# A bidirectional state scan whose matrix products go to TensorE in uncut groups on 64-row tiles, with the second direction's heads swapped

## The chip, the cores and the metric

The kernel runs on one core of a Trainium2 chip. The metric is the device time of one execution in microseconds. A core has a matrix engine (TensorE, "PE" in the profile, its weight loads "PEld"), a vector engine (DVE), a scalar engine (ACT), GpSimd (POOL), a queue engine that starts most transfers (SP), DMA engines, on-chip memory SBUF and the accumulators of TensorE, PSUM, which the program takes in banks of 512 float32 per partition.

## The reference

Two layers over 256 context and 512 latent tokens of width 1024. Layer 0 runs global attention and, beside it, bidirectional RWKV-7 time mixing on 8 heads of width 64; layer 1 runs windowed attention and a Mamba-2 scan; each layer ends with an MLP. Only layer 0's mixing stage matters here. Per head (64 wide) the time mixing runs this step over the tokens:

```
def step(S, inp):
    r_t, w_t, k_t, v_t, kk_t, a_t = inp
    sa = jnp.einsum('bhvk,bhk->bhv', S, kk_t)
    S = (S * w_t[:, :, None, :] - sa[..., None] * (kk_t * a_t)[:, :, None, :]
         + v_t[..., None] * k_t[:, :, None, :])
    return S, jnp.einsum('bhvk,bhk->bhv', S, r_t)
```

once forward and once backward (the context's final state is the latent tokens' first), with weights of its own per direction; the two `y` are added, normalised per head and gated. The attention beside it is the usual one: scores, softmax, the probabilities times the values, all in float32.

## The kernel before, in words

The recurrence is cut into chunks of 32 tokens, two chunks make a block of 64, so there are 12 blocks and 24 steps. Both directions (d = 0 forward, d = 1 backward) run through the same step, and the 8 heads lie as four pairs: pair index a = 0..3, and in a pair head h = 0 on partitions 0–63 and h = 1 on 64–127.

`prepare(b)` loads a block's operands by DMA (SP's queue: `arD` to `ari`, L958; `kbD` to `kbd`, L961; `vD` to `vm`, L965). In its `run()`, called piece by piece, each of four half-blocks (d, m) makes `z`: four matmuls of 128 rows by 128 columns (L985), one for each of two pairs and two chunks. The weights `kbd` are block-diagonal: each of the two heads' 64x64 blocks stands on its own 64 rows and 64 columns, the rest is zeros that were written once (L908/L910). DVE masks `z` twice (L991: `zk`, used for `xv`, and the first half of `z`, used for `y`), ACT copies the other half (L994). Then come two products `xv` (L1002) per block, from `zk` and `vm`, and POOL makes `ard` from `ari` by a decay factor, once per head (L976).

`step` is the recurrence: `x` = `ard` times `state` (L1026), `xs` = `x` + `xv` on DVE (L1029), `u` = the chunk's 32x32 triangular inverses `tt` times `xs` (L1036), `vu` = masked `u` + `vm`, twice on DVE (L1041), `s` = `z` times `vu` (L1051), new `state` = `s` + decayed old state on DVE (L1059). `outputs` makes `y` from `ard` times `state` (L1070) and `z` times `vu` (L1072), and adds it to `yacc`. `ard` and `zk` carry zeros or masks for the head that does not take part, so `x`, `xv` and `y` use all 128 rows and 64 columns: direction 0 on columns 0–63, direction 1 on 64–127.

Every matmul names the part of TensorE's array that it uses by rows, columns and a position: 128x128 (`z`, the scores `sc`, the transposes `pt`), 128x64 at two column positions (`xv`, `x`, `y`, `po`), 64x64 at two positions (`s`) and 32x32 at four (`u`). In float32 the trace shows two records for each such matmul and one for a transpose.

The attention of layer 0 is the other work of the stage. `attend` (L1127 on) loads `qr`, splits it into `qs` (L1136 ACT, L1137 DVE), makes scores (L1147) and probabilities (ACT L1154, L1156). `weighted` (L323, also used by layer 1's attention) transposes the probabilities four heads at a time into a bank (`pt`, L332), copies them to SBUF (`pts`, alternately DVE L335 and ACT L337) and multiplies with the values (`po`, L341).

`state_mixing` drives it: step and outputs of the recurrence, and between them pieces of `prepare` for the next block and of the attention. The order on each engine is then set by a scheduler that takes ready instructions by priority; the recurrence and the first block's preparation are issued under `tc.high_priority()`. So matmuls of one product need not stand together on TensorE: another product's can come between them.

The stage has eight PSUM banks: two for `z`, `xv` and `y` together (tag `zy`), one for `x`, `u`, `s` (`ch`), one `po`, two `pt`, two for one `sc` tile. The heaviest code ahead of the stage is the layer's input projection; behind it comes the layer's MLP. The order of these is not touched.

Of the kernel before, what the change touches and what calls it, by code (L numbers as in the profile page):

```python
# [18 lines left out]
P = 128  # L19
# [19 lines left out]
HALVES = (slice(0, 64), slice(64, 128))  # L39

# [36 lines left out]
def constants():  # L77
# [21 lines left out]
    head, slot = p // 64, (p // 32) % 2  # L99
    own = (head[:, None] == np.arange(2)[None, :])[:, :, None]  # L100
    for dr in (0, 1):
        isk = slot == dr
        sgn = np.where(isk, 1.0, -1.0).astype(f)
        if dr == 0:
            inc, exc = t[None, :] >= s[:, None], t[None, :] > s[:, None]
        else:
            inc, exc = t[None, :] <= s[:, None], t[None, :] < s[:, None]
        c.add(f"rmask{dr}", (own * inc[:, None, :] * sgn[:, None, None]).astype(f))
        c.add(f"kmask{dr}", (own * (exc & isk[:, None])[:, None, :]).astype(f))
        c.add(f"sgn{dr}", sgn)  # L110
        c.add(f"umask{dr}", (~isk).astype(f)[:, None])
# [113 lines left out]
def tile_trunk(ctx: ExitStack, tc: tile.TileContext, t: dict, out, cc: Cols, pc: Cols):  # L225
# [96 lines left out]

    def weighted(prob, vt, g, kts, o, pool):  # L323
# [5 lines left out]
        for m, kt in enumerate(kts):  # L329
            pt = psum("pt", "pt")  # L330
            for j in range(4):
                T.transpose(pt[:, P * j:P * j + P], prob[j][:, P * m:P * m + P], ident)  # L332
# [6 lines left out]
            if len(pair) == 2 or m == n - 1:  # L339
                for i, (m_, k_, w_) in enumerate(pair):  # L340
                    T.matmul(po[HALVES[i], :], lhsT=vt[:, k_, r], rhs=w_, start=m_ < 2, stop=m_ + 2 >= n, tile_position=(0, 64 * i))  # L341
# [544 lines left out]
    with ExitStack() as sb:  # L886
        psum_pool(sb, zy=(2, 1), ch=(1, 1), po=(1, 1), pt=(2, 1), sc=(1, 2))
# [25 lines left out]
        kbd = [bq.tile([P, 4, 2, P], F32, name=f"kbd{n}") for n in range(3)]  # L913
        ari = [bq.tile([P, 4, 2, P], F32, name=f"ari{n}") for n in range(3)]

# [4 lines left out]
        ard = [br.tile([P, 4, 2, 2, 64], F32, name=f"ard{n}") for n in range(5)]  # L920
        zts = [br.tile([P, 4, 2, P], F32, name=f"z{n}") for n in range(4)]
        for n in range(3):
            zero(kbd[n].rearrange("p a c n -> p (a c n)"), n > 1)
# [8 lines left out]
        A.activation(func=AF.Copy, out=dds[:, 0:7, 1, :], in_=DD[1][:, :, 6::-1].rearrange("p a n -> p n a"))  # L932
        A.activation(func=AF.Copy, out=dds[:, 7:23, 1, :], in_=DD[1][:, :, 23:7:-1].rearrange("p a n -> p n a"))
# [13 lines left out]
        def prepare(b):  # L947
# [5 lines left out]
            for d in (0, 1):  # L953
# [3 lines left out]
                kb, ar, bd = kbd[n % 3], ari[n % 3], ard[n % 5]  # L957
                nc.sync.dma_start(ar[:, :, :, 0:64], arD[d][i][:, :, c:c + P].rearrange("q a (c n) -> q a c n", c=2))  # L958
                for h in (0, 1):
                    r = HALVES[h]  # L960
                    nc.sync.dma_start(kb[r, :, :, 64 * h:64 * h + 64], kbD[d][i, r, :, c:c + P].rearrange("q a (c n) -> q a c n", c=2))  # L961
                    v = vD[64 * blk[d]:64 * blk[d] + 64, h].rearrange("(j q) a e -> q j (a e)", j=2)
                    for j in (0, 1):
                        s = 32 * (2 * h + d)
                        nc.sync.dma_start(vm[d][s:s + 32, j].rearrange("q a e -> q (a e)"), v[:, 1 - j if d else j, :])  # L965
                ld.append((kb, ar))
# [3 lines left out]
            def run():  # L970
                zks = {}
                for d in (0, 1):
                    kb, ar = ld[d]
                    for h in (0, 1):
                        r = HALVES[h]
                        G.tensor_tensor(out=ars[d][r, :, :, :, 32 * h:32 * h + 32].rearrange("p a c s t -> p (a c) s t"),  # L976
                                        in0=ar[r, :, :, 0:64].rearrange("p a c (s t) -> p (a c) s t", s=2),
                                        in1=dsel[r, b, d].rearrange("p a c -> p (a c)").unsqueeze(2).unsqueeze(3).to_broadcast([64, 8, 2, 32]),
                                        op=ALU.mult)
                    for m in (0, 1):  # L980

                        ps = psum("zy", "z")
                        for a in (0, 1):
                            for c in (0, 1):
                                T.matmul(ps[:, P * (2 * a + c):P * (2 * a + c) + P], lhsT=kb[:, 2 * m + a, c, :], rhs=ar[:, 2 * m + a, c, :],  # L985
                                         start=True, stop=True)
                        pv = ps.rearrange("p (n x) -> p n x", x=P)
                        z = zs[d][:, 2 * m:2 * m + 2].rearrange("p a c x -> p (a c) x")
                        zk = bq.tile([P, 4, 64], F32, tag="zk", name=u("zk"), bufs=4)
                        for dst, c0, nm in ((zk, 32, "kmask"), (z[:, :, 0:64], 0, "rmask")):  # L990
                            V.tensor_tensor(out=dst.rearrange("p n (h t) -> p n h t", h=2),  # L991
                                            in0=pv[:, :, c0:c0 + 32].unsqueeze(2).to_broadcast([P, 4, 2, 32]),
                                            in1=K(f"{nm}{d}").rearrange("p (h t) -> p h t", h=2).unsqueeze(1).to_broadcast([P, 4, 2, 32]), op=ALU.mult)
                        A.activation(out=z[:, :, 64:128], in_=pv[:, :, 64:128], func=AF.Copy, scale=K(f"sgn{d}"))  # L994
                        zks[d, m] = zk
                        yield
                for j in (0, 1):
                    px = psum("zy", "xv")
                    for a in range(4):
# [804 lines left out]
```

## Time and profile before

| what | value |
|---|---|
| time, three executions | 2007.61, 2008.74, 2009.6 us (median 2008.74) |
| the profiled execution's own time | 2009.51 us |
| its span | 2007.7 us, 34218 instructions |
| TensorE busy in the span | 1896.6 us, 94% |
| DVE, ACT, POOL busy | 61%, 42%, 15% |
| mean granted TensorE clock | 0.975 of full speed |

The profiled execution's 2009.51 us are its span plus 1.8 us around it; it lies 0.77 us above the median. In the window of the trace that matters, from about 350 us (the first `z`) to 625 us (the last `y`), TensorE works on the mixing stage; layer 1's attention, which shares `weighted`, lies at 1450–1610 us. A row of a timeline gives start, duration and a group of equal instructions; a row of the groups gives busy time and the mean nanoseconds of one; because matmuls overlap in the array, the distance from one group's start to the next is the time that a group costs, and not the sum of its durations.

### The profile page before, as it was taken

The numbers are of one execution on the slowest core, as the hardware profiler recorded it, in microseconds if no ns is written. First come the engines' busy times: TensorE is split into PE (matmuls) and PEld (weight loads), VectorE is DVE, ScalarE is ACT, GpSimd is POOL, SyncE is SP. The second block draws the span as 40 slices with busy tenths as digits, with TensorE's granted clock in tenths as the row PEclk, the third lists the DMA queues.
The fourth block names the chain that finished last, engine by engine and source line by source line (L and its number), as shares of the span: only waits on it lengthen the run. The fifth ranks groups of instructions, "written<-read, shape, count | busy, mean of one in ns | idle before, by whom it ended". The sixth has DMA issues, their size and how long they took to land.

```text
span 2007.7 us, 34218 instructions
## 1 busy us (share of the span) xinstructions
PE 1896.6 (94%) x13992; PEld 1545.1 (77%) x13992; DVE 1215.2 (61%) x2150; ACT 840.7 (42%) x1419; POOL 294.2 (15%) x291
## 2 busy tenths in 40 slices
PE   6999988899998999999999999899899789999997
PEld 4776756776765998888888889778578488888886
DVE  5567979775677765654544444865687464444445
ACT  3344442555544552232223224544566454333335
POOL 0000014432321520000000002310153120000001
PEclk9999998899998999999999999999999799999998
DMA  9355575742414733344444422212101133333333
GB/s 336 121 166 171 182 228 148 156 89 56 98 44 132 251 107 99 122 124 136 125 125 121 136 84 80 76 53 74 32 1 53 32 95 105 95 92 97 95 97 113
DMA packets 147884, 228.18 MB, mean 114 GB/s; under 512 B 65024, under 2 KB 102288, under 8 KB 147600
## 3 DMA queue, kind: packets, MB, share of 16 engines
q1 hardware_dynamic: 140912, 213.54, 36.1%
q10 hardware_dynamic: 5456, 7.73, 1.1%
q0 software_dynamic: 1360, 4.73, 0.7%
q8 instruction: 110, 1.80, 0.4%
q14 instruction: 46, 0.38, 0.1%
HBM read 200.00 MB, written 25.96 MB: 113 GB/s over the span
## 4 chain that ended last, share of the span: by engine, by line
PE 77%; DVE 9%; DMA 7%; ACT 3%; issue 3%; POOL 1%; SPq 0%; DVEq 0%; POOLq 0%; ACTq 0%
PE m L367 37%; PE win L367 13%; PE po L341 4%; DMA wmod<-in_wmod_dram 4%; PE pt L332 3%; PE z L985 2%; DVE wlo L280 2%; PE sc L1147 2%; PE wout L1718 1%; PE wout L1302 1%; PE s L1051 1%; PE mod L405 1%; PE lora L653 1%; PE z L1560 1%; DVE junk L1319 1%
## 5 line engine op out<-in xcount | busy, mean ns | idle before, releaser
L279 ACT ACTIVATE whi<-wraw 128x1024 fp32r<-128x1024 f32 x214 | 226.4, 1059 | 678.0 <-PE m L367 561.0
L280 DVE TENSOR_TENSOR wlo<-wraw,whi 128x1024 fp32r<-128x1024 f32 x214 | 264.4, 1236 | 212.2 <-ACT whi L279 209.4
L367 PE MATMUL m<-hh,whi 128*128 128x512 f32 (+1 forms) x816 | 239.3, 344 | 4.9 <-ACT relu L1241 2.4
L367 PE MATMUL m<-hl,whi 128*128 128x512 f32 (+1 forms) x816 | 241.2, 343 | 0.2 <-POOL hl L503 0.2
L367 PE MATMUL m<-hh,wlo 128*128 128x512 f32 (+1 forms) x816 | 241.3, 344 | 0.0
L367 PE MATMUL m<-dl,whi 128*128 128x256 f32 (+1 forms) x832 | 240.7, 341 | 0.0
L367 PE MATMUL m<-dh,whi 128*128 128x256 f32 (+1 forms) x832 | 238.6, 342 | 1.7 <-DVE xl L1223 1.6
L367 PE MATMUL m<-dh,wlo 128*128 128x256 f32 (+1 forms) x832 | 239.8, 341 | 0.1
L367 PEld LDWEIGHTS m<-dh,whi 128*128 128x128 f32 x832 | 153.3, 188 | 23.9 <-DVE xl L1223 4.9
L367 PEld LDWEIGHTS m<-hh,whi 128*128 128x128 f32 x816 | 152.1, 188 | 24.7 <-ACT relu L1241 2.8
L471 POOL TENSOR_TENSOR acc<-acc,nsq 128x256 f32<-128x256 f32 x42 | 42.8, 1027 | 865.8 <-ACT nsq L470 861.0
L367 PEld LDWEIGHTS m<-hl,whi 128*128 128x128 f32 x816 | 153.6, 188 | 19.4 <-POOL hl L503 0.4
L367 PEld LDWEIGHTS m<-dl,whi 128*128 128x128 f32 x832 | 153.8, 188 | 19.0
L367 PEld LDWEIGHTS m<-dh,wlo 128*128 128x128 f32 x832 | 153.7, 188 | 18.9 <-DVE wlo L280 0.3
L367 PEld LDWEIGHTS m<-hh,wlo 128*128 128x128 f32 x816 | 153.4, 188 | 19.0 <-DVE wlo L280 0.3
L367 PE MATMUL win<-hl,whi 128*128 128x512 f32 (+1 forms) x512 | 162.3, 348 | 4.7 <-POOL hl L503 3.5
L367 PE MATMUL win<-hh,whi 128*128 128x512 f32 (+1 forms) x512 | 162.3, 362 | 2.7 <-ACT hh L498 2.7
L367 PE MATMUL win<-hh,wlo 128*128 128x512 f32 (+1 forms) x512 | 160.2, 345 | 0.0
L1319 DVE SCALAR_TENSOR_TENSOR junk<-wmod,crow 128x1024 f32<-128x1024 f32 x64 | 78.5, 1226 | 118.5 <-DMA wmod<-in_wmod_dram 117.9
L1223 DVE SCALAR_TENSOR_TENSOR xl<-m,modT,xl 128x512 f32<-128x512 f32 (+1 forms) x144 | 97.4, 686 | 72.3 <-PE m L367 72.3
L367 PEld LDWEIGHTS win<-hh,whi 128*128 128x128 f32 x512 | 95.4, 194 | 33.6 <-issue 15.7
L367 PEld LDWEIGHTS win<-hl,whi 128*128 128x128 f32 x512 | 98.5, 193 | 22.9 <-issue 5.7
(413 smaller groups left out, 3560.0 us busy)
## 6 DMA issues: line engine op xcount, KB each, us to landing
wraw<-in_w_dram SPq DMA_DIRECT2D x136, 512.0 KB, 3.6
wmod<-in_wmod_dram SPq DMA_DIRECT2D x96, 512.0 KB, 4.2
wraw<-in_wout_dram SPq DMA_DIRECT2D x40, 512.0 KB, 3.7
wraw<-in_win_dram SPq DMA_DIRECT2D x35, 512.0 KB, 4.4
arD<-ar SPq DMA_DIRECT2D x8, 768.0 KB, 4.5
kbD<-kb SPq DMA_DIRECT2D x8, 768.0 KB, 6.5
ari<-arD SPq DMA_DIRECT2D x24, 256.0 KB, 3.9
kbd<-kbD SPq DMA_DIRECT2D x48, 128.0 KB, 3.9
```

The costliest lines, as they stand in the source:

```text
L279: A.activation(out=hi, in_=src, func=AF.Copy)
L280: (lo_eng or V).tensor_tensor(out=lo, in0=src, in1=hi.bitcast(F32), op=ALU.subtract)
L332: T.transpose(pt[:, P * j:P * j + P], prob[j][:, P * m:P * m + P], ident)
L341: T.matmul(po[HALVES[i], :], lhsT=vt[:, k_, r], rhs=w_, start=m_ < 2, stop=m_ + 2 >= n, tile_position=(0, 64 * i))
L367: T.matmul(part(ps, s), lhsT=a[:, c], rhs=row(b, k, s), start=first and j == 0 and q == 0, stop=last and j == n - 1 and q == 2)
L405: T.matmul(ps[r:r + 32, :], lhsT=cs[:, k, :], rhs=wm[:, c], start=k == 0, stop=k == KT - 1, tile_position=(0, r))
L471: (V if k == KT - 1 else eng).tensor_tensor(out=at(acc, s), in0=at(acc, s), in1=at(sq, s), op=ALU.add)
L653: T.matmul(ps[s][d][:, 0:s[1]], lhsT=LORA[wname][r, P * p:P * p + P], rhs=src[r, tokens(s)], start=True, stop=True, tile_position=(64 * d, 0))
L985: T.matmul(ps[:, P * (2 * a + c):P * (2 * a + c) + P], lhsT=kb[:, 2 * m + a, c, :], rhs=ar[:, 2 * m + a, c, :], start=True, stop=True)
L1147: T.matmul(ps[:, cols2(s)], lhsT=qs[:, 2 * j + g, :], rhs=kx[:, g, s[0]:s[0] + s[1]], start=m == 0, stop=m == 1)
L1223: V.scalar_tensor_tensor(out=xs, in0=part(ps, s), scalar=mod(l, which, m, s[2]), in1=xs, op0=ALU.mult, op1=ALU.add)
L1319: V.scalar_tensor_tensor(out=junk, in0=wm, scalar=1.0, in1=crow[:, :, v], op0=ALU.mult, op1=ALU.mult, accum_out=modT[:, l, n, v:v + 1])
```

## The change

A helper `group()` is added. A product's matmuls issued through its `put` stand on TensorE one behind another, uncut: after the first, each is issued at high priority and with an order-only dependency on the one before. It is used for `z`, `xv`, `x`, `u`, `s`, `y`, `sc` and, in `weighted`, for the four transposes of one `pt` and for a pair of `po`. Inside a group the operand that is made last comes first (the fourth head's transpose first, direction 1 first, and so on).

The heads of direction 1 are swapped: the operands of (head h, direction d) lie on rows 64·(h XOR d). With that, each product uses only its own 64 rows:

- `z`: 16 matmuls of 64x64, at the four quadrants of the array, in place of 8 of 128x128 for both directions of a half-block m. The directions write two banks, `pz[0]` and `pz[1]`.
- `xv`, `x`, `y`: 16 matmuls (`y`: 32) of 64 rows by 32 columns, at two row and four column positions, in place of 8 (16) of 128x64.
- `u` and `s`: as many as before and of the same tiles, in another order. `y` now runs all of `z` times `vu` first and `ard` times `state` behind it.
- `zk` is gone, `z` has one mask operation; `kb` and `ard` hold no zeros, and the zeroing of `kbd` and `ard` is gone. `kb` is loaded by one DMA per block and direction in place of two; `ard` is loaded by two further DMAs from `arD` and multiplied in place by one POOL operation in place of two. Two small ACT copies of the decay become four.
- PSUM banks: `z` two of its own, one for `xv`, `y` and `yt`, one `ch`, one `po`, one `pt`, two for `sc`. Eight `prob` buffers in place of five, six `ard` of half the width in place of five.

```diff
+    def group():
+        last = []
+        def put(f, *args, **kw):
+            with tc.high_priority() if last else ExitStack():
+                ins = f(*args, **kw)
+            if last:
+                tc.add_manual_dep(ins.ins, last.pop().ins.name, mybir.DependencyInfo(mybir.DependencyClass.NoSync, mybir.DependencyReason.DATA),
+                                  reason="group")
+            last.append(ins)
+        return put
...
-            for j in range(4):
-                T.transpose(pt[:, P * j:P * j + P], prob[j][:, P * m:P * m + P], ident)
+            put = group()
+            for j in (3, 2, 1, 0):
+                put(T.transpose, pt[:, P * j:P * j + P], prob[j][:, P * m:P * m + P], ident)
...
-        psum_pool(sb, zy=(2, 1), ch=(1, 1), po=(1, 1), pt=(2, 1), sc=(1, 2))
+        psum_pool(sb, z=(2, 1), zy=(1, 1), ch=(1, 1), po=(1, 1), pt=(1, 1), sc=(1, 2))
...
-        for n in range(5):
-            zero(ard[n].rearrange("p a c s n -> p (a c s n)"), n > 1)
...
-                    nc.sync.dma_start(kb[r, :, :, 64 * h:64 * h + 64], kbD[d][i, r, :, c:c + P].rearrange("q a (c n) -> q a c n", c=2))
+                nc.sync.dma_start(kb.rearrange("q a c n -> q a (c n)"), kbD[d][i][:, :, c:c + P])
...
+                for h in (0, 1):
+                    nc.sync.dma_start(bd[HALVES[h ^ d]].rearrange("q a c s t -> q a (c s t)"), arD[d][i, HALVES[h], :, c:c + P])
...
-                        ps = psum("zy", "z")
-                                T.matmul(ps[:, P * (2 * a + c):P * (2 * a + c) + P], lhsT=kb[:, 2 * m + a, c, :], rhs=ar[:, 2 * m + a, c, :],
-                                         start=True, stop=True)
+                    pz = [psum("z", "z") for _ in (0, 1)]
+                    put = group()
+                            for h, d in HD[::-1]:
+                                put(T.matmul, pz[d][HALVES[h ^ d], w:w + P], lhsT=kb[HALVES[h], 2 * m + a, c, :], rhs=ar[HALVES[h], 2 * m + a, c, :],
+                                             start=True, stop=True, tile_position=(64 * h, 64 * (h ^ d)))
...
-                        T.matmul(px[64 * d:64 * d + 64, 64 * a:64 * a + 64], lhsT=ars[d][:, a, cl[d], 1, :], rhs=state[:, d, a, :],
-                                 start=True, stop=True, tile_position=(0, 64 * d))
+                    for h, d in HD:
+                        q = 2 * d + h
+                        put(T.matmul, px[32 * q:32 * q + 32, 64 * a:64 * a + 64], lhsT=ars[d][HALVES[h ^ d], a, cl[d], 1, :], rhs=state[HALVES[h ^ d], d, a, :],
+                                     start=True, stop=True, tile_position=(64 * (h ^ d), 32 * q))
```

Here `HD` is `((0, 0), (1, 0), (1, 1), (0, 1))`, the order of (h, d) in a group.

How the orders differ is seen at two places. The first is TensorE in the middle of the stage, at the third block; the names are those of the text above, with buffer numbers, and "x8" counts equal instructions in a row. Before:

```order
L985 MATMUL z_4223<-ari_3269,kbd_3266 128x128 x4
L1036 MATMUL u_4146<-xs_4144,tt_3309 32x64 x8
L1036 MATMUL u_4146<-xs_4144,tt_3310 32x64 x4
L1036 MATMUL u_4146<-xs_4144,lor 32x64 x4
L1147 MATMUL sc_3380<-kh,qs_3317 128x256
L1147 MATMUL sc_3380<-kl,qs_3317 128x256
L1072 MATMUL y_4193<-vu_4163,z_3286 64x64
L985 MATMUL z_4239<-ari_3269,kbd_3266 128x128 x4
L1051 MATMUL s_4167<-vu_4163,z_3286 64x64 x8
L1051 MATMUL s_4167<-vu_4165,z_3287 64x64 x8
L332 MATMUL pt_3362<-cst,prob_3357 128x128
L332 MATMUL pt_3369<-cst,prob_3357 128x128
```

The two `z` groups of direction 1 stand there, between them `u` and a score tile, two transposes for each of two `pt` banks, and single `y` matmuls between other products. After the change, where the same kinds of work meet (every row of a group now carries the helper's line L330; the `z` rows are the end of a group of eight such rows):

```order
L330 MATMUL z_4719<-ari_3272,kb_3269 64x128 x2
L330 MATMUL z_4718<-ari_3271,kb_3268 64x128 x2
L330 MATMUL s_4255<-vu_4253,z_3291 64x64 x8
L330 MATMUL s_4255<-vu_4251,z_3290 64x64 x8
L330 MATMUL pt_3419<-cst,prob_3414 128x128
L330 MATMUL pt_3419<-cst,prob_3404 128x128
L330 MATMUL pt_3419<-cst,prob_3394 128x128
L330 MATMUL pt_3419<-cst,prob_3384 128x128
L330 MATMUL sc_3445<-kh,qs_3441 128x256
L330 MATMUL sc_3445<-kl,qs_3441 128x256
L330 MATMUL y_4281<-vu_4253,z_3291 32x64 x2
```

`z_4719` and `z_4718` are the two directions' banks, `s` follows without a cut, and all four transposes of one `pt` stand together.

The second place is DVE at the start of the stage, from the last transposes of the inverses (`lor`) on. Before:

```order
L781 STREAM_TRANSPOSE lor<-abm_2182 64x1024
L782 STREAM_TRANSPOSE lor<-abm_2182 64x1024
L1041 SCALAR_TENSOR_TENSOR vu_3844<-u_3827,cst,vm_3271 128x256
L1041 SCALAR_TENSOR_TENSOR vu_3846<-u_3827,cst,vm_3273 128x256
L1137 TENSOR_TENSOR qs_3317<-qr_3314,qs_3317 64x1024
L1137 TENSOR_TENSOR qs_3443<-qr_3440,qs_3443 64x1024
L991 TENSOR_TENSOR zk_3901<-z_3896,cst 128x256
L991 TENSOR_TENSOR z_3286<-z_3896,cst 128x4x64
```

After:

```order
L798 STREAM_TRANSPOSE lor<-abm_2182 64x1024
L799 STREAM_TRANSPOSE lor<-abm_2182 64x1024
L1164 TENSOR_TENSOR qs_3315<-qr_3312,qs_3315 64x1024
L1009 TENSOR_TENSOR z_3289<-z_3776,cst 128x4x64
L1009 TENSOR_TENSOR z_3288<-z_3775,cst 128x4x64
L1164 TENSOR_TENSOR qs_3441<-qr_3438,qs_3441 64x1024
L1177 TENSOR_REDUCE st_3322<-sc_3319 128x1
L1179 TENSOR_SCALAR st_3322<-st_3322,sq_99 128x1
L1183 RECIPROCAL st_3322<-st_3322 128x1
L1009 TENSOR_TENSOR z_3291<-z_3929,cst 128x4x64
L1009 TENSOR_TENSOR z_3290<-z_3928,cst 128x4x64
L1061 SCALAR_TENSOR_TENSOR vu_3868<-u_3851,cst,vm_3274 128x256
```

The split of the first queries (`qs`) has moved ahead of the second half-block's mask (`z_3289<-z_3776`, `z_3288<-z_3775`), a second split and three operations of the first score tile (`st`) ahead of the next block's masks, and these ahead of the first `vu`. On TensorE the last matmuls of that next `z` group and the first `u` alternate one by one there.

More of the change, by code (lines that the diff above doesn't have):

```diff
@@ L98, in constants @@
     t = np.arange(32)
[L99 to L100 removed]
+    slot = (p // 32) % 2
     for dr in (0, 1):
@@ L910, in zero @@
                 A.activation(out=x, in_=ident[:, 0:1].to_broadcast([P, x.shape[-1]]), func=AF.Copy, scale=0.0)
-        kbd = [bq.tile([P, 4, 2, P], F32, name=f"kbd{n}") for n in range(3)]
+        kbs = [bq.tile([P, 4, 2, 64], F32, name=f"kb{n}") for n in range(3)]
         ari = [bq.tile([P, 4, 2, P], F32, name=f"ari{n}") for n in range(3)]
@@ L1004, in run @@
+                    for a in range(3, -1, -1):
+                        for h, d in HD[::-1]:
+                            c, q, r = 1 - j if d else j, 2 * d + h, HALVES[h ^ d]
+                            put(T.matmul, px[32 * q:32 * q + 32, 64 * a:64 * a + 64], lhsT=zs[d][r, a, c, 32:64], rhs=vm[d][r, j, a, :],
+                                         start=True, stop=True, tile_position=(64 * (h ^ d), 32 * q))
                     xv = bq.tile([P, 256], F32, tag="xv", name=u("xv"), bufs=4)
@@ L1032, in step @@
             pu = psum("ch", "u")
-            for a, d, h in hd:
-                q, w = 2 * d + h, 32 * (2 * h + 1 - d)
-                g, k = divmod(NCH * a + idx[d], 32)
-                T.matmul(pu[w:w + 32, 64 * a:64 * a + 64], lhsT=tt[g][32 * q:32 * q + 32, :, k], rhs=xs[32 * q:32 * q + 32, 64 * a:64 * a + 64],
-                         start=True, stop=True, tile_position=(32 * q, w))
+            put = group()
+            for a in range(4):
+                for h, d in HD:
+                    q, w = 2 * d + h, 32 * (2 * (h ^ d) + 1 - d)
+                    g, k = divmod(NCH * a + idx[d], 32)
+                    put(T.matmul, pu[w:w + 32, 64 * a:64 * a + 64], lhsT=tt[g][32 * q:32 * q + 32, :, k], rhs=xs[32 * q:32 * q + 32, 64 * a:64 * a + 64],
+                                 start=True, stop=True, tile_position=(32 * q, w))
             vu = []
@@ L1065, in outputs @@
             py = psum("zy", "y")
+            cl = (j, 1 - j)
+            put = group()
             for a in range(4):
-                o = [py[64 * d:64 * d + 64, 64 * a:64 * a + 64] for d in (0, 1)]
-                if state is not None:
-                    for d, c in enumerate((j, 1 - j)):
-                        T.matmul(o[d], lhsT=ars[d][:, a, c, 0, :], rhs=state[:, d, a, :], start=True, stop=False, tile_position=(0, 64 * d))
-                for d, c in enumerate((j, 1 - j)):
-                    T.matmul(o[d], lhsT=zs[d][:, a, c, 0:64], rhs=vu[d][:, a, :], start=state is None, stop=True, tile_position=(0, 64 * d))
+                for h, d in HD[::-1]:
+                    q, r = 2 * d + h, HALVES[h ^ d]
+                    put(T.matmul, py[32 * q:32 * q + 32, 64 * a:64 * a + 64], lhsT=zs[d][r, a, cl[d], 0:32], rhs=vu[d][r, a, :],
+                                 start=a == 0, stop=state is None and a == 3, tile_position=(64 * (h ^ d), 32 * q))
+            for a in range(4) if state is not None else ():
+                for h, d in HD[::-1]:
+                    q, r = 2 * d + h, HALVES[h ^ d]
+                    put(T.matmul, py[32 * q:32 * q + 32, 64 * a:64 * a + 64], lhsT=ars[d][r, a, cl[d], 0, :], rhs=state[r, d, a, :],
+                                 start=False, stop=a == 3, tile_position=(64 * (h ^ d), 32 * q))
             for d in (0, 1):
@@ L1142, in attend @@
                     ps = psum("sc", "sc")
+                    put = group()
                     for s in SEGS:
```

81 lines of the change are left out of this document (36 added, 45 removed).

## The prediction

> **What bounds the kernel now.** The page comes first: its span and the chain of waits, followed back from the end.
>
> ```profile
> span 2007.7 us, 34218 instructions
> PE 77%; DVE 9%; DMA 7%; ACT 3%; issue 3%; POOL 1%; SPq 0%; DVEq 0%; POOLq 0%; ACTq 0%
> ```
>
> TensorE sets most of the end. The mixing stage is then read by itself, from busy times by window (PE, PEld, DVE, ACT, POOL, granted clock, DMA share), with layer 1's attention as the second row.
>
> ```profile
> 370.00:625.00 255.00, 249.41 (x3701) 183.13 (x3700) 176.20 (x410) 139.99 (x276) 71.11 (x64) 0.99 0.34 75
> 1450.00:1610.00 160.00, 139.06 (x808) 101.33 (x808) 101.89 (x196) 95.75 (x228) 52.38 (x60) 0.93 0.09 27
> ```
>
> In the stage TensorE works 249 of 255 us at a clock of 0.99; DVE has 79 us to spare. The waits of PE in that window, longest first, and the largest groups:
>
> ```profile
> PE z L985 <- ACT z L994: 2.3, 1, 2.3
> PE sc L1147 <- ACT prob L1154: 1.0, 2, 0.8
> ...
> L985 PE MATMUL z<-ari,kbd 128*128 128x128 f32 x344 | 50.6, 288 | 2.8 <-ACT z L994 2.3 <-ACT yacc L1080 0.5
> L332 PE MATMUL pt<-cst,prob 128*128 128x128 f32 x204 | 38.1, 290 | 0.0
> L1072 PE MATMUL y<-vu,z 128*64 128x64 f32 x368 | 34.6, 232 | 0.6 <-DVE vu L1041 0.5
> L1070 PE MATMUL y<-state,ard 128*64 128x64 f32 x368 | 31.0, 234 | 0.2 <-ACT z L994 0.2
> ```
>
> PE hardly waits, so the stage lasts as long as PE's own queue of matmuls. Could the recurrence take over once PE has less to do? Its other links are these:
>
> ```profile
> L1029 DVE TENSOR_TENSOR xs<-x,xv 128x256 f32<-128x256 f32 x23 | 9.7, 420 | 4.2 <-PE x L1026 2.3 <-ACT xv L1005 1.3
> L1041 DVE SCALAR_TENSOR_TENSOR vu<-u,cst,vm 128x256 f32<-128x256 f32 x48 | 20.8, 475 | 2.8 <-PE u L1036 2.8
> L1059 DVE TENSOR_TENSOR state<-s,old 128x512 f32<-128x512 f32 x22 | 15.2, 690 | 10.4 <-PE s L1051 10.0 <-issue 0.3
> ```
>
> The price of PE's groups comes from a stretch of the timeline; what counts is the distance from one start to the next.
>
> ```profile
> 404.99 1.16 PE L985 MATMUL z<-ari,kbd 128*128 128x128 f32 x8
> 406.08 0.69 PE L1026 MATMUL x<-state,ard 128*64 128x64 f32 x16
> 406.69 0.44 PE L332 MATMUL pt<-cst,prob 128*128 128x128 f32 x2
> 406.96 1.06 PE L985 MATMUL z<-ari,kbd 128*128 128x128 f32 x8
> 407.78 0.36 PE L1147 MATMUL sc<-kh,qs 128*128 128x256 f32 x1
> 407.98 0.28 PE L1147 MATMUL sc<-kl,qs 128*128 128x256 f32 x1
> 408.19 0.57 PE L1036 MATMUL u<-xs,tt 32*32 32x64 f32 x24
> 408.58 0.29 PE L1036 MATMUL u<-xs,lor 32*32 32x64 f32 x8
> 408.81 0.44 PE L332 MATMUL pt<-cst,prob 128*128 128x128 f32 x2
> ...
> 410.79 1.15 PE L1051 MATMUL s<-vu,z 64*64 64x64 f32 x32
> 411.87 0.38 PE L1147 MATMUL sc<-kh,qs 128*128 128x256 f32 x1
> ```
>
> A step of the recurrence is x 0.61, xs 0.42, u 0.62, two vu 0.95, s 1.08, state 0.69: 4.4 us, and perhaps 5.9 with a hand-over of some 0.25 at each of six links (an estimate). Times 24 that is 105 to 142 us of 255, so the recurrence has over 100 us of room.
>
> From the same rows: z costs 406.08 − 404.99 = 1.09 us between products of another tile shape, and 407.78 − 406.96 = 0.82 next to products of its own shape. The difference of 0.27 belongs to two changes of the array's tiling, **0.135 us each**.
>
> **The change, part by part.**
>
> *z.* Before: 48 groups of 8 records, 0.82 us without the tiling changes. After: 24 groups of 32 records. If the four quadrants of a pass run together, a group has 8 passes of four, still 128 columns wide, and costs the same 0.82. So 48 × 0.82 = 39.4 us become 19.7: **−19.7**. This rests on two things. Quadrants in different rows and columns run together: s does it above (32 records in 1.08, less 0.135 to leave: about 0.06 for each two). But two z quadrants also share columns from two row halves, which no product of the stage does. The nearest rows are the LoRA products of 64 rows, in two windows before the stage:
>
> ```profile
> 212.38 0.70 PE L653 MATMUL lora<-ad,lor 64*128 64x256 f32 x4
> 213.01 0.38 PE L367 MATMUL win<-hl,whi 128*128 128x256 f32 x1
> ...
> 229.26 0.70 PE L653 MATMUL lora<-wd,lor 64*128 64x256 f32 x2
> 229.89 0.62 PE L405 MATMUL mod<-wmod,cs 128*32 128x512 f32 x2
> ```
>
> Four records take 0.63 us, two take 0.63. The four are two row halves over the same columns, into different banks: they ran together. Bounds: −19.7 (together) and 0 (one half after the other); I take the first, since the separate banks of z make the same case.
>
> *xv, x, y.* Twice as many records of 64x32. Before, two column halves run together: 16 records in 0.61, less 0.135, or 0.06 for each two. After, four tiles at two row halves and four column strips. The nearest row is u: its four tiles differ in rows and columns, write one bank, and 32 records take 408.81 − 408.19 = 0.62. I take the same time per product as now: **0**. The other bound is one row half after the other, in the rivals.
>
> The Trainium skill speaks against this (TensorEngine Tiling (Array Packing), "Gotcha 1: PSUM Pressure"): different row tiles write to different banks and cannot use one bank at once. By that rule x, xv and y, whose row halves share a bank, would run at half speed, while z with its banks apart would gain. The trace disagrees for u, four row strips into one bank at 0.62 us; no run here shows it for 64 rows.
>
> *Tiling changes.* Counted along both orders from the first xv to the last x: 306 before, 269 after. y is cut into 24 pieces in place of 84, pt 56 in place of 74; z, xv, x and y now bring a fourth shape, and about 22 changes come from z and u alternating at the start. −37 × 0.135 = **−5.0**. Bounds −8 and −2, as the fixed cost of a change between 64-row shapes isn't shown.
>
> *Fewer banks.* pt has one bank in place of two, and xv and y share one. A bank is free when its copy is done:
>
> ```profile
> L335 DVE COPY pts<-pt 128x512 f32<-128x512 f32 x25 | 17.2, 689 | 19.4 <-PE pt L332 19.3
> L337 ACT ACTIVATE pts<-pt 128x512 f32<-128x512 f32 x25 | 14.8, 591 | 20.2 <-PE pt L332 20.1
> ```
>
> So the next pt group can start some 0.95 us (0.6 to 0.7 plus about 0.25 of hand-over) after the last one's end. In the new order s and a score tile, or x and y, mostly lie between; the nearest pairs have about 0.75 us, and two xv groups often have only a score tile of 0.42 between them against some 0.6. At 0.2 for a dozen pt pairs and 0.2 to 0.3 for some five xv pairs, this costs **+3**. What waits behind is PE's whole queue, the recurrence too. Bounds 0 and +15 (0.27 for all 56 pt groups).
>
> *Start of the stage.* On DVE and ACT before:
>
> ```profile
> 363.93 0.88 DVE L1041 SCALAR_TENSOR_TENSOR vu<-u,cst,vm 128x256 f32<-128x256 f32 x2 [0.43 <-PE u L1036]
> 364.83 1.22 DVE L1137 TENSOR_TENSOR qs<-qr,qs 64x1024 fp32r<-64x1024 f32 x1
> 366.52 2.06 DVE L1137 TENSOR_TENSOR qs<-qr,qs 64x1024 fp32r<-64x1024 f32 x1 [0.47 <-ACT qs L1136]
> ...
> 307.98 2.00 ACT L910 ACTIVATE kbd<-cst 128x1024 f32<-128x1024 f32 x2 [6.79 <-PE gate L756]
> 309.88 1.98 ACT L910 ACTIVATE ard<-cst 128x1024 f32<-128x1024 f32 x2
> ```
>
> The first vu now stands behind both qs splits (3.3 us), a score tile's operations and four masks, so the first state comes about 5 us later, of which PE fills a part with scores and z. Against it the zeroing is gone (3.9 us of ACT, ahead of copies that the stage's loads wait for). Together **+2**; bounds −4 and +6.
>
> *Layer 1.* po's pairs stand together there too: 22 fewer tiling changes, 3.0 us at most, in a stage where PE is idle for 21 of 160 us: **−1**; bounds −3 and +2.
>
> *At nothing.* DVE loses 48 masks, and POOL half of its `ard` operations:
>
> ```profile
> L976 POOL TENSOR_TENSOR ard<-ari,dsel 64x512 f32<-64x512 f32 x42 | 45.0, 1072 | 52.3 <-PE y L1070 29.7 <-DMA ari<-arD 19.9 <-PE z L985 1.0
> ```
>
> Neither bounds the stage. SP issues 22 more transfers and about 6.3 MB more, where the DMA share is 0.34; loads run a block (some 21 us) ahead, which covers them. Without that cover each late load would cost its own few us, 12 blocks of them, so I count this under the rivals.
>
> The sum: −19.7 − 5.0 + 3 + 2 − 1 = −20.7. The profiled execution took 2009.51; the median of the runs is 0.77 lower. 2008.7 − 20.7 = **1988 us**.
>
> **Rivals.**
>
> *Waits take the gain.* The single pt bank and the shared bank cost their upper bound, +15 in place of +3, or ard's loads come late (1 us for each of 12 blocks): 1988 + 12 to 15, about 2001. For it: PE's queue is in order, and the gaps are near the copies' length. Against it: only the nearest pairs are short.
>
> *Slower: row halves in one bank don't run together.* 94 groups (x 23, xv 24, y 24 and 23) would each take a second 0.47 us (0.61 less 0.135): +44, so 1988 + 44 = 2032. It decides from 0.22 us per group (20.7 / 94), that is from 0.69 for 32 records without the changes. For it: the rule cited. Against it: u's 0.62.
>
> *z's quadrants don't run together.* Then z costs 39.4 us as before and the change does not do what it says: 2008. For it: it is not seen within the stage. Against it: the LoRA rows.
>
> *More gain.* No waits, the zeroing's removal reaching the stage, layer 1's full 3 us: −24.7 − 3 − 4 = −31.7, or 1977.
>
> **How the numbers follow.** Chances: the forecast 0.56, waits 0.17, slower 0.08, z without gain 0.08, more gain 0.11. The terms' bounds put the forecast's own case at about 1978 to 1998; the range 1974 to 2007 takes in the waits and most of the greater gain, and leaves out the two cases on the other side. Within 0.2% (4 us, about what a measurement of this kernel can tell from no change) falls most of z without gain and the end of the waits: 0.08. Faster: 0.56 + 0.11 + 0.15 = 0.82. Slower: 0.10.
>
> **What would show it.** z: a group of 32 records at about 0.82 us from start to start, and not 1.6. x: 32 records at about 0.61 with its changes; 1.0 would show the slower case. Waits: PE's waits on pts copies and on xv's copy in the stage, some 3 us in sum and not 15. Start: the first vu near 369 us and PE idle ahead of it. The stage from the first z to the last y should last about 20 us less than its 275; layer 0's MLP should keep its length. The prediction fails if row halves serialise, or if PE's idle time in the stage grows past 25 us.

## The result, and the profile after

The changed kernel takes 2025.68 us (median; 2021.63 to 2027.07), the kernel before 2008.38: a ratio of 1.0082 with a 95% interval of 1.0065 to 1.010. Forecast were 1988 us, with a range of 1974 to 2007. The change makes the kernel 17 us slower.

The page of the changed kernel, its span and the chain that ended last:

```profile
span 2024.3 us, 37863 instructions
PE 81%; DVE 7%; DMA 4%; ACT 4%; issue 2%; POOL 1%; SPq 0%; ACTq 0%; POOLq 0%; DVEq 0%
```

That row alone would say that TensorE still sets the end. The busy times by window tell more (PE, PEld, DVE, ACT, POOL, granted clock, DMA share). The stage is cut in two: from the first z to the last y, and from there to the end of the output projection's first half. First the kernel before, then the changed one:

```profile
350.00:625.00 275.00, 264.42 (x3872) 196.22 (x3873) 194.68 (x445) 146.42 (x286) 79.16 (x69) 0.97 0.37 82
625.00:669.00 44.00, 36.10 (x233) 29.09 (x234) 33.72 (x51) 21.78 (x30) 13.82 (x12) 0.88 0.76 249
```

```profile
345.00:643.00 298.00, 251.23 (x5787) 179.47 (x5787) 180.08 (x407) 151.33 (x294) 52.65 (x46) 0.89 0.39 95
643.00:689.00 46.00, 31.34 (x211) 29.29 (x212) 30.48 (x46) 17.32 (x23) 14.27 (x11) 0.74 0.71 229
```

PE's busy time, weighted at each moment with the clock granted then, is its work at full speed; busy time less that is what the lower clock cost; the rest of the window is idle. (The products of the rows above give the work to within 2 us, and to within 4 us in the runs below, because the mean clock of a window takes in its idle stretches.)

| PE in the stage, us | length | work | lower clock | idle |
|---|---|---|---|---|
| before | 319 | 290 | 10 | 19 |
| changed | 344 | 248 | 35 | 61 |

So the change did take work from TensorE, 42 us and not the 25 forecast. Idle time grew by 42 us and the lower clock by 25, and these decide. The stage is 25 us longer; it begins 5 us earlier, and the rest of the program is about 3 us shorter.

PE's longest waits in the changed stage between 370 and 645 us, by their sums; between 370 and 625 us the kernel before had 5.3 us of waits in all:

```profile
PE z L330 <- DMA kb<-kbD: 9.2, 5, 3.6
PE sc L330 <- ACT prob L1182: 5.5, 10, 1.3
PE x L330 <- DVE state L1080: 4.6, 5, 1.4
PE xv L330 <- ACT xv L1022: 4.3, 2, 3.1
PE u L330 <- DVE xs L1047: 2.8, 2, 1.9
```

The matmuls of 64 rows run side by side as forecast. The timeline where the clock is full:

```profile
600.06 1.10 PE L330 MATMUL z<-ari,kb 64*64 64x128 f32 x32
601.10 0.46 PE L330 MATMUL u<-xs,tt 32*32 32x64 f32 x16
...
605.84 0.65 PE L330 MATMUL y<-vu,z 64*32 64x64 f32 x32
606.31 0.63 PE L330 MATMUL y<-state,ard 64*32 64x64 f32 x32
606.77 0.63 PE L330 MATMUL x<-state,ard 64*32 64x64 f32 x32
607.33 1.08 PE L330 MATMUL po<-pts,vtok 128*64 128x512 f32 x4
```

Both directions of z, 32 records, take 1.04 us from start to start, with another tile shape on either side; before, one direction took 1.09 like that, and 0.82 with no other shape beside it. y takes 0.47 and 0.46 for 32 records of 64x32 (forecast 0.47). Both kinds of overlap, two row halves over the same columns into two banks (z) and two row halves into one bank (x, y), are there.

The largest sum is waits on a load. TensorE and SP's queue at the second block's end, where z of the second half-block ends at about 377 us:

```profile
375.26 1.99 PE L330 MATMUL z<-ari,kb 64*64 64x128 f32 x32
377.04 1.31 PE L330 MATMUL s<-vu,z 64*64 64x64 f32 x32
...
384.30 2.10 PE L330 MATMUL z<-ari,kb 64*64 64x128 f32 x32 [3.56 <-DMA kb<-kbD]
```

```profile
377.28 1.35 SPq L974 DMA_DIRECT2D ari<-arD  x2
378.68 1.37 SPq L975 DMA_DIRECT2D kb<-kbD  x2
```

The load of the next operands is issued just when that z ends, and lands after PE needs it. There are three `kb` and three `ari`, and a block takes two of each. A z group now reads both directions' operands to its last matmul, so of the next block only one direction finds a free buffer. After the wait the group itself takes twice as long, 2.10 us in place of 1.10: the clock has fallen. It is at half behind five of PE's six waits on `kb` in the stage (10.8 us in sum).

And the start: z and u alternate for twelve rounds at half clock, until 373.5 us.

```profile
361.32 1.08 PE L330 MATMUL z<-ari,kb 64*64 64x128 f32 x10 [1.63 <-DMA kb<-kbD]
362.33 0.42 PE L330 MATMUL u<-xv,tt 32*32 32x64 f32 x2
362.68 0.69 PE L330 MATMUL z<-ari,kb 64*64 64x128 f32 x2
```

The first vu comes at 373.64 in place of 363.93.

### The profile page after: what moved, and what is told of

Same layout as the page of the kernel before. It is cut to its first block, busy times and chain, and to the rows that moved or that the text cites. A ratio compares the mean times of both kernels' runs of the same rounds, so it can differ in the third digit from the quotient of the medians.

```text
span 2024.3 us, 37863 instructions
## 1 busy us (share of the span) xinstructions
PE 1868.4 (92%) x15880; PEld 1532.2 (76%) x15880; DVE 1198.8 (59%) x2102; ACT 838.8 (41%) x1417; POOL 257.5 (13%) x263
## 4 chain that ended last, share of the span: by engine, by line
PE 81%; DVE 7%; DMA 4%; ACT 4%; issue 2%; POOL 1%; SPq 0%; ACTq 0%; POOLq 0%; DVEq 0%
PE m L384 44%; PE win L384 13%; PE pt L330 2%; PE po L330 2%; PE wout L1330 2%; PE wout L1746 2%; PE z L330 2%; DMA kb<-kbD 2%; PE lora L670 1%; PE sc L330 1%; PE z L1588 1%; PE mod L422 1%; PE s L330 1%; DMA wraw<-in_win_dram 1%; PE y L330 1%
```

## The experiments

**Undoing or doing one half.** First the groups, the layout, the loads and the start, each by itself.

The changed kernel without groups:

```diff
         def put(f, *args, **kw):
-            with tc.high_priority() if last else ExitStack():
-                ins = f(*args, **kw)
...
+            return f(*args, **kw)
```

> The changed kernel, but every product's matmuls are issued one by one again, so the scheduler may cut them; tiles, swapped heads, banks and loads stay. Theory A (late loads: kb and ari have three buffers, and z of both directions reads two at once, so the next load starts only when the last z has ended; 10.8 us of PE waits in the changed kernel and a halved clock after each) expects that cutting changes little: 2025.7 within 5 us, with kb waits still there. Theory C (uncut groups leave PE without filler behind a wait: sc, x, xv, u, s and po waits of some 24 us, and the low clock after them) expects most of the loss to go: about 2000 to 2008 us, these waits under 8 us. Either way the 12 alternations of z and u at the start should go, worth up to 9 us by theory B.

Measured: 2020.67 us, ratio 1.005 (1.0035 to 1.0065). That is 5.0 us less, the edge of what theory A allows; waits on kb are still 12.9 us, and the start has no alternation. Most of the loss is not the groups'.

The kernel before, with groups alone (the same `put` around its own products):

> The kernel before with the uncut groups alone (all products it has, the last operand's first in xv, s and pt); tiles, heads, banks and loads as before. Theory C expects a slower kernel than before, by 10 us or more (2018 and up), with new PE waits on prob, state, xs. If grouping by itself does no harm, fewer tiling changes give 2002 to 2008 us.

Measured: 1988.94 us, ratio 0.9895 (0.988 to 0.9909). Theory C falls: groups are a gain of 20 us, more than either expectation. The windows of that kernel, cut at its own last y:

```profile
349.00:603.00 254.00, 235.49 (x3849) 188.42 (x3850) 191.79 (x442) 141.75 (x279) 80.45 (x71) 0.96 0.41 92
603.00:651.00 48.00, 37.83 (x260) 30.80 (x261) 34.66 (x54) 25.91 (x37) 13.41 (x11) 0.89 0.70 220
```

Work is 261 us where it was 290: 29 us less. Counted along its order there are 209 tiling changes in place of 306, but these are only half of it. PE's work by product, as the distance from each record's start to the next without idle time and lower clock, falls most for `po`, from 42.7 to 27.9 us for the same 112 records. Of 25 pairs of `po` in the window 350 to 625 us of the kernel before, 13 were cut apart:

```profile
487.75 1.07 PE L341 MATMUL po<-pts,vtok 128*64 128x512 f32 x2
488.75 0.66 PE L332 MATMUL pt<-cst,prob 128*128 128x128 f32 x4
...
493.81 1.08 PE L341 MATMUL po<-pts,vtok 128*64 128x512 f32 x4
494.82 0.39 PE L1147 MATMUL sc<-kh,qs 128*128 128x256 f32 x1
```

One column half alone, two records, takes 1.00 us, and both halves together, four records, 1.01. In groups all pairs stand together. The other 14 us, spread over the 97 changes, are 0.14 each.

The changed kernel with four buffers:

```diff
...
-                kb, ar, bd = kbs[n % 3], ari[n % 3], ard[n % 6]
+                kb, ar, bd = kbs[n % 4], ari[n % 4], ard[n % 6]
```

> The changed kernel with four buffers in place of three for kb and ari. Theory A expects PE's waits on kb (10.8 us, 6 times) to go to under 2 us, the clock in the stage to rise, and 2008 to 2014 us. If the late loads only hide other waits (theory C), those take their place and the time stays within 5 us of 2025.7.

Measured: 1995.08 us, ratio 0.992 (0.9899 to 0.994). The gain is 30.6 us, more than theory A expected. No wait on kb is left among PE's waits; the longest between 370 and 617 us, and the windows:

```profile
PE sc L330 <- ACT prob L1182: 7.7, 13, 1.8
PE s L330 <- DVE vu L1061: 6.0, 7, 1.2
PE u L330 <- DVE xs L1047: 5.8, 6, 1.8
...
344.00:617.00 273.00, 227.76 (x5762) 164.94 (x5764) 182.45 (x411) 150.08 (x294) 54.03 (x46) 0.93 0.42 102
617.00:664.00 47.00, 32.16 (x241) 29.87 (x234) 30.38 (x45) 17.17 (x22) 14.05 (x11) 0.72 0.68 224
```

One buffer more also changes the scheduler's order: z and u no longer alternate at the start, and the first vu is back at 363.5. So the 30.6 us are the loads and the start together. But look at the idle time: 60 us, as in the changed kernel. Work is down to 239 us, and the stage is 320 us long, no shorter than the 319 of the kernel before. This kernel beats the one before only outside the stage, by some 6 us at its begin and as much behind it. PE's work in the stage by product, counted as above:

| PE's work, us | z | po | y | pt | xv, x | s, u, sc | rest |
|---|---|---|---|---|---|---|---|
| before | 50.0 | 42.7 | 34.5 | 33.7 | 28.5 | 74.5 | 26.3 |
| before, with groups | 48.2 | 27.9 | 31.3 | 27.7 | 25.2 | 74.3 | 26.8 |
| changed | 33.0 | 29.1 | 23.3 | 29.3 | 30.7 | 75.6 | 26.6 |
| changed, four buffers | 26.9 | 28.3 | 23.3 | 31.1 | 27.8 | 74.8 | 26.3 |

The start alone, with three buffers (the second block's first z behind the first u):

```diff
...
-                    put = group()
+                    put = group(first_u if b == 1 and m == 0 else ())
...
```

> The changed kernel with one order added: the second block's first z group stands behind the first u group, so the two no longer alternate. Theory B (the start: 12 pairs of z and u at 0.97 us each, 12.2 us from 361.3 to 373.5 where about 3 are needed) expects the first vu near 365 us in place of 373.6 and 2014 to 2019 us. If PE only waits elsewhere for the time gained (for the late kb), the time falls by under 4 us.

Measured: 2021.57 us, 4.1 us less, ratio 1.0056 (1.0041 to 1.0071). The first vu came at 363.0, 10.6 us earlier, as theory B said, but the time lies between the two expectations; the kb waits were still 8.2 us and the mean step of the recurrence, from one s group to the next, rose from 11.76 to 12.21 us. Most of what the start gives is lost in the steps behind it.

**Together, and with the groups taken out.**

> The changed kernel with four kb and ari buffers and with the second block's first z group behind the first u. If the late loads and the start add up, 1995.1 less the 4.1 us that the order at the start gave alone, so 1989 to 1993 us. If the stage is by now bound by something else (the recurrence behind PE waits on xs, vu and prob, or the bare end), it stays at 1993 to 1998 us.

Measured: 1993.51 us, ratio 0.9922 (0.9901 to 0.9943), within the spread of the run with four buffers alone, which had already mended the start. In its profile the stage is 312 us long, with 239 us of work and 57 idle.

> The changed kernel with four kb and ari buffers, its matmuls not grouped. Theory C (uncut groups leave PE without filler) expects it under 1990 us, below the 1995.1 of the grouped one, as 2020.7 is below 2025.7 with three buffers. If grouping saves tiling changes in this layout as it did in the kernel before (20 us there), it is at 2005 us or more.

Measured: 2009.93 us, ratio 1.001 (0.9996 to 1.0024). With the loads on time, groups gain 15 us in the new layout too: 302 tiling changes without, 228 with. Without groups the new layout, loads on time, is no faster than the kernel before, and with groups no faster than the kernel before with groups.

**The end of the stage.** In the run with four buffers and the new start PE's last product of the attention comes at 601 us, ahead of the last step's s at 604, and behind the last y PE waits 8.1 us in one piece for the normalisation. Handing the attention out later (the first of two runs; fewer pieces per step, as the texts below say, are cut from the excerpt):

```diff
...
-        for _ in range(40):
+        for _ in range(8):
```

> As the run with four buffers and the new start order, and the attention handed out later: 8 pieces in place of 40 ahead of the recurrence and four in place of five per step, so that some of it is left for the end. Theory D (the attention that covers PE is used up by the 22nd step, the last steps and the final normalisation run bare: 8.1 us of PE wait in one piece and 16 us without work ahead of the output projection) expects the wait on the last yacc gone and 6 to 10 us less than that run. If the end is bound by the recurrence itself, the time stays within 3 us of it.

> As the run with the attention handed out later, but later still: 20 pieces ahead and three per step, so that 12 are left behind the recurrence. Theory D expects the last yacc wait to be filled and 1984 to 1990 us. If what is covered at the end is missing in the middle (PE then waits on the recurrence there), it stays at 1992 to 1998 us as in that run.

Measured: 1995.02 us (ratio 0.9933, 0.9908 to 0.9957) and 1993.73 us (0.9926, 0.9907 to 0.9945), against 1993.51 without. In the first the wait was 6.9 us in place of 8.1, so the end was hardly covered. In the second it was 2.8, and nothing came of it: the steps have less attention between them and are no shorter, 10.75 us as against 10.77. Theory D falls as a way to the lost time.

**The banks.** One pt bank in the grouped kernel before:

```diff
-        psum_pool(sb, zy=(2, 1), ch=(1, 1), po=(1, 1), pt=(2, 1), sc=(1, 2))
+        psum_pool(sb, zy=(2, 1), ch=(1, 1), po=(1, 1), pt=(1, 1), sc=(1, 2))
```

> The kernel before with uncut groups, and one pt bank in place of two. The prediction's term for fewer banks was +3 us for pt and xv together (bounds 0 and +15). If it holds, 1989 to 1994 us; a single pt bank that costs 0.27 per group would give 2000 to 2004 us.

Measured: 2022.88 us, ratio 1.007 (1.0043 to 1.0098): 34 us slower, outside every bound. The windows, cut at its last y:

```profile
350.00:583.00 233.00, 218.58 (x3739) 176.19 (x3741) 174.22 (x408) 124.08 (x249) 80.09 (x70) 0.96 0.43 94
583.00:686.00 103.00, 70.11 (x381) 48.79 (x378) 53.18 (x89) 45.24 (x68) 14.32 (x11) 0.75 0.37 115
```

PE hardly waits for the pt bank itself (4.4 us). The recurrence ends 20 us earlier than with two banks, but attention is left over, and runs alone behind it: 103 us, 33 of them idle, at a clock of 0.75. In this kernel a bank too few shifts which of the two streams comes last.

The opposite in the new layout, two pt banks and one z bank:

> The run with four buffers and the new start order, with the banks dealt otherwise: one z bank, in which the two directions follow each other (two quadrants at a time, so z costs 0.82 us per direction as before the change, some 20 us of PE more), and two pt banks. Theory E (the single pt bank holds up the attention, which then leaves PE idle: 57 us of idle time in the stage) expects the idle time to fall by at least the 20 us that z costs, and 1980 to 1993 us. If idle time has other causes (the start, the recurrence's own chain, the bare end), the 20 us show: 2005 to 2015 us.

Measured: 2003.03 us, ratio 0.9972 (0.9959 to 0.9984), between the two expectations. z one direction at a time cost some 18 us of work; idle time fell by 3 us only. So the single pt bank is not what keeps the new layout idle, as far as a run can say that has one z bank less as well.

**y's order in the layout before.**

> The kernel before with uncut groups, and y's products in the change's order: all of z times vu first, ard times state behind it, so that y's group is not cut by its wait for vu. Along its order there are 182 tiling changes in place of the 209 of the grouped kernel before. At the 0.29 us per change that the grouped kernel showed (28.5 us of work for 97 changes) this saves 8 us of PE: 1979 to 1984 us. If PE's work no longer sets the end there, it stays at 1986 to 1992 us.

Measured: 2008.14 us, ratio 0.9997 (0.9984 to 1.0011), a miss. The 182 tiling changes came, and PE's work fell by 4 us, which is 0.14 for each of the 27 and not 0.29. But idle time rose from 29 to 45 us (waits of s on vu, of xv on zk), and the mean step from 10.32 to 11.53 us. These waits suggest that y's state part had filled the gap in front of vu, and that uncut behind vu it leaves that gap open. The changed kernel has this order of y too, and no run undoes it there; what it costs in the new layout is not known.

**What the recurrence needs by itself.** Its own length was measured by leaving the attention out.

> The run with four buffers and the new start order, without the attention of layer 0: its scores, probabilities and products are left out and zeros are written in their place, so the recurrence with its preparation runs alone. It measures the length of the recurrence by itself, from the first z at 345 us to the last y. If the recurrence has the room that the prediction gave it (4.4 to 5.9 us per step), the last y comes near 490 us. If its chain is as long as the stage (theory F: the recurrence itself bounds the new layout), the last y comes after 560 us.

Measured, one run: 1958.79 us; the last y came at 578.6, theory F's side. From the first s group to the last, a step took 9.32 us on average, where the whole kernel had 10.77. In the stage, counted as above, PE worked 150 us and was idle for 93.

> The kernel before without the attention of layer 0 (left out as in the run of the new layout without it). If the recurrence with its preparation has the same length in both layouts, a step takes about 9.3 us on average, as there. If the new layout lengthened it, 8.5 us or less. If the old layout's dearer PE work shows even alone, 10 us or more.

Measured, one run: 1930.70 us; a step took 7.56 us. The recurrence alone is 1.8 us longer per step in the new layout, though its PE work is smaller. The s groups of both, first the new layout, then the one before, with the start of the first and of the last record:

```profile
L330 PE MATMUL s<-vu,z x736: 218/218/366, 367.4 to 573.3; 64*64 64x64 f32 x184
```

```profile
L1051 PE MATMUL s<-vu,z x736: 218/218/366, 372.3 to 539.6; 64*64 64x64 f32 x184
```

Over 22 steps that is 9.36 and 7.60 us with the last group's own length in it, 9.32 and 7.56 from group start to group start. A step of the new layout that holds a z product, from its x to its s:

```profile
444.66 1.08 PE L330 MATMUL x<-state,ard 64*32 64x64 f32 x32
445.66 1.75 PE L330 MATMUL z<-ari,kb 64*64 64x128 f32 x32
447.35 0.65 PE L330 MATMUL xv<-vm,z 64*32 64x64 f32 x32
450.90 0.69 PE L330 MATMUL z<-ari,kb 64*64 64x128 f32 x4 [2.90 <-ACT z L1012]
452.10 1.97 PE L330 MATMUL z<-ari,kb 64*64 64x128 f32 x28 [0.51 <-ACT z L1012]
454.00 1.08 PE L330 MATMUL xv<-vm,z 64*32 64x64 f32 x32
455.01 0.75 PE L330 MATMUL u<-xs,tt 32*32 32x64 f32 x18
...
457.18 1.97 PE L330 MATMUL s<-vu,z 64*64 64x64 f32 x32 [1.09 <-DVE vu L1065]
```

Between x and u stand two z groups and two xv groups. The second z needs both z banks free and waits for the copies of the first; u waits behind it in PE's queue, and x to u takes 10.4 us, the longest of the run, in part at half clock. In the layout before, a step without z, from the same view of the run without attention:

```profile
434.91 0.68 PE L1026 MATMUL x<-state,ard 128*64 128x64 f32 x15
435.67 0.72 PE L1002 MATMUL xv<-vm,zk 128*64 128x64 f32 x15
...
437.27 0.50 PE L1036 MATMUL u<-xs,tt 32*32 32x64 f32 x18 [0.70 <-DVE xs L1029]
```

Here 2.4 us, and 1.7 in most steps that have one z group in between. Over 22 steps x to u takes 4.2 us on average in the new layout, 4.6 to 10.4 where both z groups stand in between, as against 1.9 in the layout before. From u to the next s it is 2.0 and 2.5, from s to x 3.1 and 3.2. So the 1.8 us are lost between x and u. The remaining two runs separate the halves of the change.

> The kernel before with uncut groups, without the attention of layer 0 (scores, probabilities and products left out, zeros written). Alone, a step of the recurrence took 7.56 us in the old layout without groups and 9.32 in the new one with groups and four buffers. If the groups lengthen it (theory C, PE's queue held up behind an uncut product), 8.5 us or more here. If the new layout does (z of both directions at once, one bank for xv and y), it stays at 7.3 to 8.0 us.

> The new layout with four buffers, not grouped, without the attention. If the groups lengthen the step, about 7.6 us here; if the new layout does, 8.8 us or more, with waits of z on z's copy and of xv on xv's copy as in the grouped run (21.7 and 5.6 us).

Measured, one run each: 1930.67 us with 7.60 us per step, and 1950.39 us with 8.91. In the layout before, the groups do not lengthen the step; the new layout with its banks does, and there the groups add at most 0.4 us (8.91 to 9.32, where the second has the new start as well). Which part of the layout does it, both directions' z in one product or the banks, no run separates.

**A shorter chain.** s with direction 0 first, in the new layout, in the grouped layout before, and with the later hand-out:

```diff
-            for d, a in ((d, a) for d in (1, 0) for a in range(4)):
+            for d, a in ((d, a) for d in (0, 1) for a in range(4)):
```

> The run with four buffers and the new start order, with s's group in the other order: direction 0 first, whose vu is made first, where the change puts the last one (direction 1) first. Theory F (the recurrence bounds the new layout) expects the second vu's 0.44 us to fall out of each of 23 steps, so the last y some 10 us earlier and 1983 to 1987 us. If PE or the attention bounds the stage, it stays at 1991 to 1996 us.

> The kernel before with uncut groups, with the same change of s's order. There PE works 262 of 302 us in the stage, so theory F expects less of it than in the new layout: 1984 to 1989 us. 1978 us or less would mean that the recurrence bounds the old layout as much as the new.

> The run with the attention handed out later still, with s's direction 0 first. Theory F expects the same 10 us as without the later hand-out, and the filled end keeps its place: 1980 to 1986 us. If it stays at 1991 us or more, the order of s isn't what the steps wait for.

Measured: 1985.90 us (ratio 0.9881, 0.9861 to 0.9901), 1984.50 us (0.9877, 0.9854 to 0.99) and 1990.80 us (0.9906, 0.9889 to 0.9923), so 8, 4 and 3 us less than without; the intervals of the last two overlap those of their kernels without it, so only the first is clear. The first falls into theory F's numbers, but not by its reason: in its profile the mean step is 10.79 us as against 10.77, and the last y comes at 610.5 as against 610.3. That profile is of its slowest execution, 1990.1 us, and where the 8 us lie stays open. The second lies in its expectation, with a mean step of 10.31 as against 10.32; the third falls between both of its own. The first two are the fastest kernels of the study and beat both the kernel before and the changed one.

## Why the prediction was wrong

- **"At nothing": the loads.** This step failed by the most. They were said to run a block ahead, which covers them. The buffers were not counted against it: three, with a product that now holds both directions' until its end. This cost, with the start that hangs on it, 30.6 us (the run with four buffers), of the 38 between forecast and measurement. The rival with late loads had the right place, at 1 us per block, and no falling clock. (SP issues 24 more transfers, not 22: 48 for `ard`, 24 fewer for `kb`.)
- **"So the recurrence has over 100 us of room."** This step failed too, and four buffers do not mend it. It added the links of a chain (4.4, at most 5.9 us) and left out what PE's in-order queue puts between them. Alone, with nothing of the attention, a step took 7.56 us in the old layout and 9.32 in the new. The rule "PE hardly waits, so the stage lasts as long as its queue" held for the kernel before, not for one with 42 us less work: with four buffers PE has 239 us of work, and the stage still takes 320 us, or 312 with the new start. The prediction's own sign of failing, idle time of PE past 25 us in the stage, came true: 47 us from the first z to the last y.
- **Fewer banks, +3.** Mis-sized. In the changed kernel PE's waits on xv's and pt's copies are some 5 us. But the price of a bank is not the wait for it: in the layout before, with groups, one pt bank less cost 34 us, by leaving the attention to the end. In the new layout a second one, at the cost of a z bank, showed no such gain.
- **Start, +2.** The first vu came 9.7 us later (forecast 5) and the first z 4.9 us earlier. Mending it alone gave 4.1 us.
- **Tiling changes, −5.** The size was right by luck. The 0.27 was halved as the price of two changes, but a distance with another shape on either side holds the part of one change that falls to its end and the part of another that falls to its start, so the price of one. In z's rows that is 0.27. Around x and po it is 0.15, near what the halving gave: a group of x takes 0.47 us between products of its own shape (below), 0.57 with another behind, 0.51 with another in front, and 0.62 with both.

```profile
433.28 0.64 PE L1026 MATMUL x<-state,ard 128*64 128x64 f32 x16
433.75 1.51 PE L1002 MATMUL xv<-vm,zk 128*64 128x64 f32 x30
```

- **Left out: pairs of po that run together.** The prediction booked the groups for their tiling changes alone. The table by product gives the 42 us of work: z 17, po 14, y 11, pt 4, with 2 us more for xv and x and 1 for s, u and sc. po's 14 come from both column halves working at once, and have no term in the sum.
- **z, −19.7.** Right. z's work falls by 17 us in the changed kernel, and by 23 with four buffers, where z no longer alternates with u at the start. Its groups are now 24 of 1.04 us, with their changes, in place of 48.
- **xv, x, y, 0.** Right: 0.47 and 0.46 for 32 records. The rival of halves that do not overlap did not come true. Nor did the rule of the Trainium skill on row tiles in one bank (TensorEngine Tiling (Array Packing), "Gotcha 1: PSUM Pressure"); the measurement decides.
- **Layer 1, −1.** The program behind the stage is 3 us shorter; of what, no run separates.
- The slower rivals each had one mechanism in TensorE's array. The true one, waits that take more than the whole gain because PE is no longer the bound and its clock falls while it waits, was the rival "waits take the gain", priced at 12 to 15 us where idle time and clock cost 67 more than before.

## What to carry to other kernels

Before a gain on the busiest engine is booked, find the length of the next limit by leaving the other stream out, not by adding up the links of its chain: an in-order queue adds what stands between them. When a product is made to read more operands at once, count the buffers of each again: with three buffers and two in use by one group, the load of a whole block cannot run ahead. And before a saving is put down to fewer switches, split the engine's work by product: half of what the groups saved came from pairs that now run side by side.

## What the runs showed of the hardware

- A change of the array's tiling cost 0.15 us around x and po of 128x64 (x 0.47 us without, 0.62 with another shape on either side; four records of po 0.86 and 1.01) and 0.27 around z of 128x128. The Trainium skill (TensorEngine Tiling (Array Packing), "Key Properties") says that changing the tiling mode drains TensorE; the trace agrees.
- Two column halves of 128x64 run at once when their matmuls stand together: a group of po takes 1.00 us with one half and 1.01 with both.
- Four 64x32 tiles at two row halves and four column strips write one bank at the same time: 32 records in 0.46 to 0.47 us, 15 ns each, as long as 16 records of 128x64 took before (0.47).
- In the changed kernel's recurrence all five idle stretches of PE of 2.3 us and more (2.36 to 4.64) were followed by half clock, for instance z 2.10 us in place of 1.10 after 3.56 us. Of those from 1.0 to 2.1 us four were and eight were not. Over the stage the lower clock cost the changed kernel 35 us, more than half as much as its 61 us of idle time.
